# A decoder layer on Trainium2: the first feed-forward product turned token-major in ten groups, with seven block products for eight in two of eight k pairs

## The chip, the cores and the metric

The kernel runs on one core of a Trainium2 chip. The metric is the device time of one execution in microseconds. The engines are named as in the profile: PE is TensorE (PEld its weight loads), DVE is VectorE, ACT is ScalarE, POOL is GpSimd, SP is SyncE, whose queue issues the DMAs.

## The reference

One layer over 256 tokens of 2048 channels in float32: three token-mixing branches (attention, gMLP, S5) from one input projection, merged by gates, an output projection and a layer norm; then the feed-forward half that the change is about:

```python
gate_f, up = jnp.split(x @ w_ffn_in[l], 2, axis=-1)       # x (256, 2048), w_ffn_in (2048, 2 x 5632)
f = (jax.nn.silu(gate_f) * up) @ w_ffn_out[l]             # w_ffn_out (5632, 2048)
x = _layer_norm(ALPHA * x + f, ln2_g[l], ln2_b[l])
```

## The kernel before

**Split numbers.** Each float32 factor is cut into a high part (rounded to fp32r) and a low part (the remainder), and a product is made of three fp32r products: high x high, high x low, low x high. ScalarE makes the high part of a weight block (`split_h`, L262), VectorE the remainder (`split_l`, L268). Activations are kept as tiles of 512 columns for a k block of 128 channels: 256 tokens high, then 256 tokens low (`xT`, `x1T`, `h`).

**Units.** All work with weights is a list of `Unit`s of up to 1024 weight columns (8 k blocks x 128, or 2 x 512). The loop at L1210 goes through them: split the high parts of units up to four ahead (`advance`, four buffers `wh` and four `wl`), issue the unit's products, then its `post`, deferred steps and one step of each running task, then the remainders of what was split (`remainders`), each of which lets `top_up` issue a further weight load on SP (`load`, L251; four buffers `raw`). So every engine's order is fixed by this loop: a unit's split waits for the unit four before it to be multiplied, and a load for the remainder that frees its buffer. Engines work through their queues in order.

**Two forms of product.** `wide` (L79, L80) gives the output channel-major: the weights are the stationary tile, the activations move; for each k block one product of 512 columns (high weights x high and low tokens) and one of 256 (low weights x high tokens). `tall` (L165 to L167) gives it token-major: 128 tokens of an activation are the stationary tile and 512 columns of weights move; three products of 512 columns for each k block and half of the tokens. `w_v`, `w_o` and the second feed-forward product are `tall`; the gates and the first feed-forward product are `wide`.

**First feed-forward product.** 44 blocks f of 128 channels, each with a gate and an up tile of 16 k blocks, in two units each. The first four tiles run in `quad_tiles` (L108, L111) while the first layer norm ends, the other 84 through `wide`. `post_f1` adds the two halves of the bank (ScalarE, VectorE), makes silu x up and writes the split result into `h_tile(f)`: `h0` (f below 12, tag x24) or `h1` to `h10` (three f each, tag s6). `x1T` (tag t32) is the layer norm's result.

**Second.** Four column groups of `tall` over 44 k blocks, with `h` as the stationary tile. `ln2_load` runs ahead of its first unit and loads two rows of the norm, 1 MB each once spread over the partitions, into tag t32, where `x1T` was. The residual is read from `z` (tag t16, 2 MB), which the first layer norm left there.

**Places.** The pool's tags follow one another in each partition's memory, so a tile's start is fixed by what stands before it. By the built program xT, x1T, z, raw, wh, wl and h0 start 1632 bytes past a multiple of 2048 (32 past a multiple of 64), all tiles of tag s6 (m, h1 to h10, ...) 1728 past one, which is a multiple of 64. PSUM has four banks of tag mm and four of tag sd.

## Time and profile before

| | us |
|---|---|
| three runs, median (lowest, highest) | 1602.92 (1602.57, 1603.49) |
| the profiled execution | 1604.32 |
| its span, first to last instruction | 1602.6 |
| PE, DVE, ACT, POOL busy | 1580.8, 931.0, 763.8, 559.9 |
| first feed-forward product, `wide` tiles | 868.7 to 1343.5 |
| second feed-forward product | 1343.6 to 1589 |

The terms of a change are stage times within the span; the execution has 1.7 us around it, and the median of the runs stands 1.4 us below the profiled one. A row of the timeline is start, duration, engine, line, operation; products are pipelined, so the time of one is the distance between starts, not its duration.

### The profile page before, as it was taken

What the parts mean: (1) busy time and instruction counts of PE and PEld (TensorE: products, weight loads), DVE (VectorE), ACT (ScalarE), POOL (GpSimd) and SP (SyncE); (2) the same over time, 40 slices, a digit from 0 to 9 for tenths busy, and PEclk for the clock granted to TensorE, in tenths of its full rate; (3) what the DMA queues carried; (4) which work ended last, traced back from release to release, by engine and by line L of the source; (5) the groups of instructions that cost most, each with busy time, mean ns of one, the idle gap of its engine ahead of it and who ended that gap; (6) DMA issues with size and microseconds to landing.
All of it is one profiled execution on the core that took longest, in us unless ns stands there. A gap on an engine that the chain in (4) does not pass through costs nothing.

```text
span 1602.6 us, 24113 instructions
## 1 busy us (share of the span) xinstructions
PE 1580.8 (99%) x9094; PEld 1366.3 (85%) x9094; DVE 931.0 (58%) x1232; ACT 763.8 (48%) x1040; POOL 559.9 (35%) x1147
## 2 busy tenths in 40 slices
PE   8999999999999999999999999999999999999996
PEld 7888888898999998889789888888888888888885
DVE  5444555556855565469667556565555555445455
ACT  5444434456544444475444545554444544333342
POOL 7569999933999999203011000000000000000002
PEclk9999999999999999999999999999999999999998
DMA  8575557655656555557863565555555556666663
GB/s 275 176 251 186 187 203 207 155 148 188 211 188 198 194 184 194 178 164 209 286 222 118 190 193 184 184 184 184 186 185 192 183 193 237 204 187 192 186 188 101
DMA packets 106492, 307.50 MB, mean 192 GB/s; under 512 B 27567, under 2 KB 28079, under 8 KB 106120
## 3 DMA queue, kind: packets, MB, share of 16 engines
q1 hardware_dynamic: 106280, 305.82, 59.7%
q8 instruction: 71, 1.16, 0.3%
q14 instruction: 45, 0.37, 0.1%
q0 software_dynamic: 96, 0.15, 0.0%
HBM read 303.78 MB, written 5.53 MB: 193 GB/s over the span
## 4 chain that ended last, share of the span: by engine, by line
PE 94%; DVE 3%; DMA 1%; ACT 1%; issue 0%; POOL 0%; SPq 0%; POOLq 0%; ACTq 0%
PE ps_mm L79 40%; PE ps_mm L80 20%; PE ps_mm L165 9%; PE ps_mm L166 9%; PE ps_mm L167 9%; DVE wl L268 1%; PE ps_mm L857 1%; PE ps_mm L858 1%; PE ps_mm L856 1%; PE ps_sd L522 1%; PE ps_sd L691 1%; PE ps_mm L108 0%; PE ps_mm L111 0%; PE ps_sd L670 0%; DMA ln<-in_ln_g_dram 0%
## 5 line engine op out<-in xcount | busy, mean ns | idle before, releaser
L268 DVE TENSOR_TENSOR wl<-raw,wh 128x1024 fp32r<-128x1024 f32 (+1 forms) x544 | 654.2, 1227 | 167.1 <-ACT wh L262 166.6
L262 ACT ACTIVATE wh<-raw 128x1024 fp32r<-128x1024 f32 (+1 forms) x544 | 556.7, 1024 | 369.1 <-PE ps_mm L167 171.6
L79 PE MATMUL ps_mm<-xT,wh 128*128 128x512 f32 x1344 | 480.6, 400 | 6.6 <-ACT wh L58 5.9
L79 PE MATMUL ps_mm<-x1T,wh 128*128 128x512 f32 x1344 | 474.9, 399 | 0.0
L80 PE MATMUL ps_mm<-xT,wl 128*128 128x256 f32 x1344 | 378.9, 282 | 0.5 <-DVE wl L268 0.5
L80 PE MATMUL ps_mm<-x1T,wl 128*128 128x256 f32 x1344 | 377.5, 281 | 0.0
L79 PEld LDWEIGHTS ps_mm<-xT,wh 128*128 128x128 f32 x1344 | 254.3, 189 | 67.1 <-ACT wh L58 5.9
L79 PEld LDWEIGHTS ps_mm<-x1T,wh 128*128 128x128 f32 x1344 | 252.6, 188 | 63.0
L937 POOL TENSOR_TENSOR z<-z,ln2w 128x512 f32<-128x512 f32 (+1 forms) x4 | 5.2, 1302 | 732.5 <-ACT z L936 732.5
L80 PEld LDWEIGHTS ps_mm<-xT,wl 128*128 128x128 f32 x1344 | 256.1, 191 | 1.5 <-DVE wl L268 0.8
L80 PEld LDWEIGHTS ps_mm<-x1T,wl 128*128 128x128 f32 x1344 | 253.9, 189 | 0.0
L546 POOL TENSOR_TENSOR X<-X,t 128x48 f32<-128x48 f32 x255 | 129.1, 506 | 48.6 <-ACT X L526 48.6
L544 POOL TENSOR_TENSOR t<-s5keep,X 128x48 f32<-128x48 f32 x254 | 126.6, 498 | 44.5 <-ACT X L526 24.7
L547 POOL TENSOR_TENSOR X<-X,t 128x48 f32<-128x48 f32 x255 | 129.9, 509 | 20.0
L166 PE MATMUL ps_mm<-wl,h 128*128 128x512 f32 x340 | 134.1, 394 | 0.0
L165 PE MATMUL ps_mm<-wh,h 128*128 128x512 f32 x340 | 134.1, 394 | 0.0
L167 PE MATMUL ps_mm<-wh,h 128*128 128x512 f32 x340 | 134.1, 394 | 0.0
L1037 DVE TENSOR_TENSOR tmp<-ps_mm,tmp 128x256 f32<-128x256 f32 x88 | 37.3, 424 | 152.9 <-ACT tmp L1036 152.9
L545 POOL TENSOR_TENSOR t<-s5keep,X 128x48 f32<-128x48 f32 x254 | 108.5, 427 | 0.0
L315 ACT ACTIVATE tmp<-ps_mm,bcol 128x256 f32<-128x256 f32 x90 | 42.7, 474 | 137.6 <-PE ps_mm L80 137.4
L1036 ACT ACTIVATE tmp<-ps_mm 128x256 f32<-128x256 f32 x88 | 33.8, 384 | 151.6 <-PE ps_mm L80 151.6
L165 PEld LDWEIGHTS ps_mm<-wh,h 128*128 128x128 f32 x340 | 64.0, 188 | 15.0
(214 smaller groups left out, 1775.6 us busy)
## 6 DMA issues: line engine op xcount, KB each, us to landing
raw<-in_w_f_dram SPq DMA_DIRECT2D x264, 512.0 KB, 4.3
raw<-in_w_b_dram SPq DMA_DIRECT2D x164, 512.0 KB, 4.6
raw<-in_w_o_dram SPq DMA_DIRECT2D x32, 512.0 KB, 5.0
raw<-in_w_v_dram SPq DMA_DIRECT2D x24, 512.0 KB, 4.0
raw<-in_w_p_dram SPq DMA_DIRECT2D x32, 384.0 KB, 3.4
raw<-in_w_zv_dram SPq DMA_DIRECT2D x16, 384.0 KB, 3.6
tmp<-tab SPq DMA_DIRECT2D x64, 64.0 KB, 3.2
raw<-in_w_p_dram SPq DMA_DIRECT2D x16, 256.0 KB, 2.9
```

Of the source, the lines that this page charges most:

```text
L79: T.matmul(ps, lhsT=h[:, j * 128:(j + 1) * 128], rhs=a, start=k == 0, stop=last, skip_group_check=True)
L80: T.matmul(ps[:, 0:256], lhsT=l[:, j * 128:(j + 1) * 128], rhs=a[:, 0:256], start=False, stop=last, skip_group_check=True)
L165: T.matmul(ps[:, :n], lhsT=ah, rhs=hs, start=k == 0, stop=False)
L166: T.matmul(ps[:, :n], lhsT=ah, rhs=ls, start=False, stop=False)
L167: T.matmul(ps[:, :n], lhsT=al, rhs=hs, start=False, stop=k == total - 1)
L262: A.activation(h[:, :m], raws[n][:, :m], AF.Copy)
L268: V.tensor_tensor(l[:, :m], raws.pop(n)[:, :m], h[:, :m].bitcast(F32), op=ALU.subtract)
L315: A.activation(t, ps[:, 256:512], AF.Identity, bias=bcol[:, col:col + 1], scale=scale)
L544: G.tensor_tensor(t1, keep[:, 0], prev, op=ALU.mult)
L545: G.tensor_tensor(t2, keep[:, 1], prev[:, :, ::-1], op=ALU.mult)
L546: G.tensor_tensor(cur, cur, t1, op=ALU.add)
L547: G.tensor_tensor(cur, cur, t2, op=ALU.add)
```

## The change

Blocks f 4 to 43 (ten groups of four) are computed token-major by `seven`; f 0 to 3 stay as they were. A group has eight bank-sized results of 128 tokens x 512 channels or sums of such. In k pairs 0, 1, 2, 5, 6, 7 the eight block products (gate and up, two halves of the tokens, two k blocks) are made as in `tall`, three products each. In pairs 3 and 4 a seven-product scheme runs: VectorE makes sums of the four weight blocks (`combine`: four operations of 512 columns) and, once, of x1T's blocks (`sums`, tile `S`), and seven block products are accumulated in banks 1 to 7; `evict` after pair 4 takes out banks 1, 7, 6, 5 and `gates_` and `ups` add the rest. A pair has four units: g and u (loaded, 1024 columns), t1 (512) and tt (1024), which are sums and have no load. The banks of a group are split over tags mm and sd by turns. `turns` transposes the gated result in the next group (four transposes and one split for each half of the tokens, after its units 3 and 4). `S` takes the place of `z`, which is sent to DRAM and read back in `ln2_load`. A load now takes four runs of 1 KB from each partition's row in place of one of 4 KB. A constant `pad` of 320 bytes, and the S5 integers moved before it, make x1T, S, raw, wh, wl, h0 and all tiles of tag s6 start on multiples of 2048.

TensorE, first feed-forward product, before: weights `wh`, `wl` as stationary tile, x1T moving, by k block:

```order
L79 MATMUL ps_mm<-x1T,wh 128x512
L80 MATMUL ps_mm<-x1T,wl 128x256
L79 MATMUL ps_mm<-x1T,wh 128x512
L80 MATMUL ps_mm<-x1T,wl 128x256
L79 MATMUL ps_mm<-x1T,wh 128x512
```

The same place after, end of unit g to tt of a group's first pair (`S` the sums of x1T, ps the output bank):

```order
L1134 MATMUL ps_sd<-wh,x1T 128x512
L1135 MATMUL ps_sd<-wh,x1T 128x512
L1136 MATMUL ps_sd<-wl,x1T 128x512
L1134 MATMUL ps_mm<-wh,S 128x512
L1135 MATMUL ps_mm<-wh,S 128x512
L1136 MATMUL ps_mm<-wl,S 128x512
L1134 MATMUL ps_sd<-wh,S 128x512
L1135 MATMUL ps_sd<-wh,S 128x512
L1136 MATMUL ps_sd<-wl,S 128x512
L1134 MATMUL ps_mm<-wh,S 128x512
```

The weights have become the moving tile, and each block is three products of 512 columns.

VectorE, before, one pair of gate and up tiles (L268 the remainders of the units to come, the others the tile's end):

```order
L1037 TENSOR_TENSOR tmp_12776<-ps_mm,tmp_12776 128x256
L1046 SCALAR_TENSOR_TENSOR tmp_12779<-tmp_12779,tmp_12776 128x256
L268 TENSOR_TENSOR wl<-raw,wh 128x1024 x2
L1037 TENSOR_TENSOR tmp_12827<-ps_mm,tmp_12827 128x256
L1050 TENSOR_TENSOR tmp_12779<-tmp_12779,tmp_12827 128x256
```

VectorE, after, in a late group, from the turned halves of the group before (L66) to the remainder of tt (L301 with tt, 1024 columns):

```order
L66 SCALAR_TENSOR_TENSOR h_11065<-ps_mm,h_11065 128x2x128
L301 TENSOR_TENSOR wl<-raw,wh 128x1024
L66 SCALAR_TENSOR_TENSOR h_10709<-ps_mm,h_10709 128x2x128
L66 SCALAR_TENSOR_TENSOR h_11065<-ps_mm,h_11065 128x2x128
L301 TENSOR_TENSOR wl<-raw,wh 128x1024
L301 TENSOR_TENSOR wl<-tt,wh 128x512
L292 TENSOR_TENSOR tt<-raw 128x512
L293 TENSOR_TENSOR raw<-raw 128x4x128
L294 TENSOR_TENSOR tt<-raw 128x512
L295 TENSOR_TENSOR tt<-raw,tt 128x512
L301 TENSOR_TENSOR wl<-tt,wh 128x1024
```

The second pair's four sums (L292 to L295) stand ahead of the remainder that the first pair's tt products need.

SP, after, from the four `wide` tiles to the second product (L262 weight loads, zd the copy of z in DRAM):

```order
L262 DMA raw<-in_w_f_dram 128x1024 x12
L1101 DMA zd<-z 128x2048 x2
L262 DMA raw<-in_w_f_dram 128x4x256 x160
...
L1271 DMA z<-zd 128x2048 x2
L1275 DMA ln2w<-in_ln_g_dram 128x2048
L1275 DMA ln2w<-in_ln_b_dram 128x2048
```

z leaves ahead of the groups' loads and comes back ahead of the norm's two rows, on the one queue.

```diff
--- before.py
+++ after.py
@@ -39,6 +39,10 @@
     V, A, G, T = nc.vector, nc.scalar, nc.gpsimd, nc.tensor
 
     RAW_BUFS, HL_BUFS, AHEAD = 4, 4, 4
+    PAD = 80
+    PAIRS = (3, 4)
+    SP = len(PAIRS)
+    FIRST, LAST = 1, 10
 
     def bank(tag="mm"):
         return psp.tile([128, 512], F32, tag=tag, bufs=4, name=f"ps_{tag}")
@@ -63,8 +67,10 @@
 
 
...
@@ -247,8 +253,14 @@
 
         def load(n):
             u = units[n]
+            if u.role in ("t1", "tt"):
+                return
             r = raw_tile()
-            nc.sync.dma_start(r[:, :u.k * u.n], u.src)
+            if u.role:
+                u.pair[u.role] = r
+            dst = r[:, :u.k * u.n]
+            nc.sync.dma_start(dst if len(u.src.shape) == 2 else dst.rearrange("p (f c) -> p f c", f=u.src.shape[1]),
+                              u.src)
             raws[n] = r
 
         def split_h(n):
@@ -259,13 +271,36 @@
             else:
                 h = sb.tile([128, 1024], F32R, tag="wh", bufs=HL_BUFS, name="wh")
                 l = sb.tile([128, 1024], F32R, tag="wl", bufs=HL_BUFS, name="wl")
+            if u.role == "g" and "t" not in u.pair:
+                combine(u.pair)
+            elif u.role == "t1":
+                raws[n] = u.pair["t"][:, 0:512]
+            elif u.role == "tt":
+                raws[n] = u.pair["t"][:, 512:1536]
+                if u.pair["next"]:
+                    combine(u.pair["next"])
             A.activation(h[:, :m], raws[n][:, :m], AF.Copy)
             hl[n] = rest[n] = (h, l)
 
+        def combine(p):
+
+            p["t"] = s6([128, 1536], F32, "tt")
+            b = [p[e][:, 0:1024].rearrange("p (f k c) -> p k f c", f=4, k=2) for e in "gu"]
+            b11, b21, b12, b22 = b[0][:, 0], b[0][:, 1], b[1][:, 0], b[1][:, 1]
+            t1, t2, t4 = (p["t"][:, 512 * i:512 * i + 512].rearrange("p (f c) -> p f c", f=4) for i in range(3))
+            V.tensor_tensor(t1, b12, b11, op=ALU.subtract)
+            V.tensor_tensor(b12, b22, b12, op=ALU.subtract)
+            V.tensor_tensor(t2, b12, b11, op=ALU.add)
+            V.tensor_tensor(t4, b21, t2, op=ALU.subtract)
+
         def split_l(n):
-            m = units[n].k * units[n].n
+            u = units[n]
+            m = u.k * u.n
             h, l = rest.pop(n)
             V.tensor_tensor(l[:, :m], raws.pop(n)[:, :m], h[:, :m].bitcast(F32), op=ALU.subtract)
+            if u.role not in ("t1", "tt"):
+                pos["raw"] -= 1
 
         pos = {}
 
@@ -284,7 +319,12 @@
 
         def top_up():
             seq = pos["seq"]
-            if pos["load"] < len(seq) and pos["load"] - pos["l"] < RAW_BUFS:
+            if pos["load"] < len(seq):
+                u = units[seq[pos["load"]][0]]
+                if u.role not in ("t1", "tt"):
+                    if pos["raw"] >= RAW_BUFS:
+                        return False
+                    pos["raw"] += 1
                 load(seq[pos["load"]][0])
                 pos["load"] += 1
                 return True
@@ -301,6 +341,8 @@
...
+        s5["i"] = const.tile([128, NJ], I32, name="s5i")
+        const.tile([128, PAD], F32, name="pad")
 
 
...
         def s5_setup():
             P = s5["P"]
-            PI = sb.tile([128, NJ], I32, tag="s5i", bufs=1, name="s5i")
+            PI = s5["i"]
             keep = const.tile([128, 3, NJ, 2], F32, name="s5keep")
             bm = s6([128, 2, NJ, 32], F32, "bm")
             bb = s6([128, 2, NJ, 32], F32, "bb")
@@ -1024,7 +1066,7 @@
                     big["h0"] = sb.tile([128, 12, 512], F32R, tag="x24", bufs=1, name="h0")
                 return big["h0"][:, f, :]
             i = (f - 12) // 3
-            if (f - 12) % 3 == 0 and ("h", i) not in big:
+            if ("h", i) not in big:
                 big["h", i] = s6([128, 3, 512], F32R, f"h{i}")
             return big["h", i][:, (f - 12) % 3, :]
 
@@ -1051,6 +1093,157 @@
                     y = h_tile(f)
                     copy_split(y[:, 0:256], y[:, 256:512], w, 0.5)
             return post
+
+        def first_sums():
+
+            big["zd"] = dram.tile([128, 2, D], F32, name="zd")
+            for t in range(2):
+                nc.sync.dma_start(big["zd"][:, t, :], big["z"][:, t, :])
+            spawn(sums())
+
+        def sums():
...
+            big["S"] = sb.tile([128, 4, SP, 256], F32R, tag="t16", bufs=1, name="S")
+            for s in range(4):
+                o = big["S"][:, s]
+                copy_split(o[:, :, 0:128], o[:, :, 128:256], sr[:, s])
+                if s % 2:
+                    yield
+
...
+        def three(ps, a, h, l, start, stop):
+            T.matmul(ps, lhsT=a[0], rhs=h, start=start, stop=False)
+            T.matmul(ps, lhsT=a[1], rhs=h, start=False, stop=False)
+            T.matmul(ps, lhsT=a[0], rhs=l, start=False, stop=stop)
+
+        def seven(g):
+
+            P = {}
+            tags = ("mm", "sd") if g % 2 == 0 else ("sd", "mm")
+
+            def cols(w, j):
+                return w.rearrange("p (f k c) -> p k f c", f=4, k=2)[:, j]
+
+            def prod(n, a, h, l, start, stop):
+                if n not in P:
+                    P[n] = bank(tags[n in (1, 5, 6, 7)])
+                three(P[n], a, h, l, start, stop)
+
+            def mk(role, i):
+                def mm(h, l):
+                    z = 2 * PAIRS[i]
+                    ends = i == 0, i == SP - 1
+                    if role == "g":
+                        prod(1, act2(0, z), cols(h, 0), cols(l, 0), *ends)
+                        prod(2, act2(0, z + 1), cols(h, 1), cols(l, 1), False, False)
+                    elif role == "u":
+                        prod(7, act_s(2, i), cols(h, 0), cols(l, 0), *ends)
+                        prod(3, act_s(3, i), cols(h, 1), cols(l, 1), False, False)
+                    elif role == "t1":
+                        prod(5, act_s(0, i), h[:, 0:512], l[:, 0:512], *ends)
+                    else:
+                        prod(6, act_s(1, i), h[:, 0:512], l[:, 0:512], *ends)
+                        prod(4, act2(1, z + 1), h[:, 512:1024], l[:, 512:1024], False, False)
+                return mm
+
+            def mk8(up, i):
+                def mm(h, l):
+                    for t in range(2):
+                        for j in range(2):
+                            prod(((2, 4), (3, 8))[up][t], act2(t, 2 * i + j), cols(h, j), cols(l, j),
+                                 (i, j) == (0, 0), (i, j) == (7, 1))
+                return mm
+
+            def begin():
+                if g > FIRST:
+                    spawn(turns(g - 1))
+
+            def evict():
+                c = P["c"] = {n: tmp() for n in (1, 7, 6, 5)}
+                A.activation(c[1], P[1], AF.Copy)
+                V.tensor_tensor(c[6], P[6], c[1], op=ALU.add)
+                V.tensor_tensor(c[7], P[7], c[6], op=ALU.add)
+                V.tensor_tensor(c[6], P[5], c[6], op=ALU.add)
+                V.tensor_tensor(c[5], P[5], c[7], op=ALU.add)
+
+            def gates_():
+                c = P["c"]
+                P["w"] = [tmp(), tmp()]
+                for t, (n, m) in enumerate(((1, 2), (7, 4))):
+                    V.tensor_tensor(c[n], P[m], c[n], op=ALU.add)
+                    A.activation(P["w"][t], c[n], AF.Tanh, scale=0.5)
+
+            def ups():
+                c = P["c"]
+                for n, m in ((6, 3), (5, 8)):
+                    V.tensor_tensor(c[n], P[m], c[n], op=ALU.add)
+
+                def rest(t):
+                    w, a, b = P["w"][t], c[(1, 7)[t]], c[(6, 5)[t]]
+                    V.scalar_tensor_tensor(w, w, 1.0, a, op0=ALU.add, op1=ALU.mult)
+                    V.tensor_tensor(w, w, b, op=ALU.mult)
+                    if t == 0:
+                        later(lambda: rest(1), 0)
+                later(lambda: rest(0), 0)
+                big["w", g] = P["w"]
+
+            src = [d["w_f1"][8 * g + up:8 * g + 8:2].rearrange("f p k c -> p f k c") for up in range(2)]
+            pairs = [{} for _ in PAIRS]
+            for i, p in enumerate(pairs):
+                p["next"] = pairs[i + 1] if i + 1 < SP and g < LAST else None
+            for i in range(8):
+                s = [a[:, :, 2 * i:2 * i + 2, :].rearrange("p f k c -> p f (k c)") for a in src]
+                if i in PAIRS:
+                    e = PAIRS.index(i)
+                    pair = pairs[e]
+                    units.append(Unit(s[0], 8, 128, mk("g", e), role="g", pair=pair))
+                    units.append(Unit(s[1], 8, 128, mk("u", e), role="u", pair=pair))
+                    units.append(Unit(None, 4, 128, mk("t1", e), role="t1", pair=pair))
+                    units.append(Unit(None, 8, 128, mk("tt", e), role="tt", pair=pair,
+                                      post=evict if e == SP - 1 else None))
+                else:
+                    units.append(Unit(s[0], 8, 128, mk8(0, i), post=gates_ if i == 7 else None,
+                                      before=begin if i == 0 else None))
+                    units.append(Unit(s[1], 8, 128, mk8(1, i), post=ups if i == 7 else None))
+
+        def turns(g):
+
+            tag = "mm" if g % 2 == 0 and g < LAST else "sd"
+            for _ in range(3):
+                yield
+            for t in range(2):
+                ps = bank(tag)
+                for f in range(4):
+                    T.transpose(ps[:, f * 128:(f + 1) * 128], big["w", g][t][:, f * 128:(f + 1) * 128], ident)
+                f = 4 * g
+                while f < 4 * g + 4:
+                    n = min(4 * g + 4, 12 if f < 12 else f + 3 - f % 3) - f
+                    h_tile(f)
+                    y = big["h0"][:, f:f + n] if f < 12 else big["h", (f - 12) // 3][:, f % 3:f % 3 + n]
+                    copy_split(y[:, :, t * 128:(t + 1) * 128], y[:, :, 256 + t * 128:256 + (t + 1) * 128],
+                               ps.rearrange("p (f c) -> p f c", f=4)[:, f - 4 * g:f - 4 * g + n], 0.5)
+                    f += n
+                yield
 
...
         def ln2_load():
+            big["z"] = sb.tile([128, 2, D], F32, tag="t16", bufs=1, name="z")
+            for t in range(2):
+                nc.sync.dma_start(big["z"][:, t, :], big["zd"][:, t, :])
             w = sb.tile([128, 2, D], F32, tag="t32", bufs=1, name="ln2w")
+            spawn(turns(LAST))
             for i, nm in enumerate(("ln2_g", "ln2_b")):
                 nc.sync.dma_start(w[:, i, :], d[nm].partition_broadcast(128))
             big["ln2"] = w
@@ -1141,8 +1338,14 @@
                 f1.append(([d["w_f1"][2 * f + up, :, u * 8:(u + 1) * 8, :].rearrange("p k c -> p (k c)")
                             for u in range(2)], post_f1(f, up)))
         quad_tiles(f1[:4], act_x1, [home_x24(i) for i in range(3)] + [home_s6], ln1_hook)
-        for srcs, post in f1[4:]:
-            wide(srcs, 8, act_x1, post)
+        for i, (srcs, post) in enumerate(f1):
+            if 4 <= i < 8 * FIRST:
+                wide(srcs, 8, act_x1, post, before=first_sums if i == 4 else None)
+        for g in range(FIRST, LAST + 1):
+            seven(g)
+        for i, (srcs, post) in enumerate(f1):
+            if i >= 8 * LAST + 8:
+                wide(srcs, 8, act_x1, post)
         for g in range(4):
             tall([d["w_f2"][g, i].rearrange("p k c -> p (k c)") for i in range(22)], 2, 512, act_h, post_f2(g),
                  before=ln2_load if g == 0 else None, late=(lambda t, i: None) if g == 3 else None,
@@ -1203,7 +1406,7 @@
         for i in range(4):
             at = marks["o"] + 10 + 4 * i
             seq.insert(at + i, (first + i, at))
-        pos.update(load=4, h=4, l=4, live=4, seq=seq)
+        pos.update(load=4, h=4, l=4, live=4, raw=0, seq=seq)
         while top_up():
             pass
         marks["s5"] = spawn(s5_setup())
```

## Rows read from the trace of the kernel before

**Rows 1.** The page: busy us and instructions by engine; the chain by engine.
```profile
PE 1580.8 (99%) x9094; PEld 1366.3 (85%) x9094; DVE 931.0 (58%) x1232; ACT 763.8 (48%) x1040; POOL 559.9 (35%) x1147
...
PE 94%; DVE 3%; DMA 1%; ACT 1%; issue 0%; POOL 0%; SPq 0%; POOLq 0%; ACTq 0%
```
**Rows 2.** Both stages: us, PE, PEld, DVE, ACT, POOL busy, clock, DMA share, GB/s.
```profile
868.00:1343.00 475.00, 475.00 (x2693) 412.07 (x2692) 282.78 (x384) 238.28 (x340) 0.00 (x0) 1.00 0.58 187
1343.00:1589.00 246.00, 246.00 (x1061) 199.04 (x1059) 120.10 (x114) 93.75 (x91) 5.19 (x4) 1.00 0.61 190
```
**Rows 3.** L79: all starts in the first product; two from the gates' timeline.
```profile
L79 PE MATMUL ps_mm<-x1T,wh x1344: 395/398/403, 868.7 to 1343.3; 128*128 128x512 f32 x192
...
639.67 0.39 PE L79 MATMUL ps_mm<-xT,wh 128*128 128x512 f32 x1
...
659.78 0.39 PE L79 MATMUL ps_mm<-xT,wh 128*128 128x512 f32 x1
```
**Rows 4.** Timeline of PE: w_v, w_o, second product (h0, later h); L108.
```profile
210.19 0.39 PE L165 MATMUL ps_mm<-wh,xT 128*128 128x512 f32 x1
...
229.91 0.39 PE L165 MATMUL ps_mm<-wh,xT 128*128 128x512 f32 x1
...
784.99 0.40 PE L165 MATMUL ps_mm<-wh,m 128*128 128x512 f32 x1
...
802.57 0.39 PE L165 MATMUL ps_mm<-wh,m 128*128 128x512 f32 x1
...
1344.31 0.40 PE L165 MATMUL ps_mm<-wh,h 128*128 128x512 f32 x1
...
1359.96 0.39 PE L165 MATMUL ps_mm<-wh,h 128*128 128x512 f32 x1
...
1360.66 0.40 PE L165 MATMUL ps_mm<-wh,h 128*128 128x512 f32 x1
...
1380.34 0.40 PE L165 MATMUL ps_mm<-wh,h 128*128 128x512 f32 x1
...
847.45 2.08 PE L108 MATMUL ps_mm<-x1T,wh 128*128 128x256 f32 x16
```
**Rows 5.** Timeline of PE: four transposes between products of w_o.
```profile
837.47 0.39 PE L167 MATMUL ps_mm<-wh,m 128*128 128x512 f32 x1
837.70 0.60 PE L956 MATMUL ps_sd<-ident,z 128*128 128x128 f32 x4
838.05 0.48 PE L165 MATMUL ps_mm<-wh,m 128*128 128x512 f32 x1
838.37 0.40 PE L166 MATMUL ps_mm<-wl,m 128*128 128x512 f32 x1
```
**Rows 6.** VectorE's remainders: count, total us, mean ns; one of 512 columns.
```profile
L268 DVE TENSOR_TENSOR wl<-raw,wh 128x1024 fp32r<-128x1024 f32 x205 | 244.8, 1221 | 107.3 <-ACT wh L262 107.1
...
371.64 0.69 DVE L268 TENSOR_TENSOR wl<-raw,wh 128x512 fp32r<-128x512 f32 x1
```
**Rows 7.** Start of the second product: SP, ACT, and a window's row.
```profile
1347.60 0.42 SPq L1078 DMA_DIRECT2D ln2w<-in_ln_g_dram  x1
...
1349.33 1.06 ACT L262 ACTIVATE wh<-raw 128x1024 fp32r<-128x1024 f32 x1 [1.66 <-PE ps_mm L167]
1352.05 1.06 ACT L262 ACTIVATE wh<-raw 128x1024 fp32r<-128x1024 f32 x1 [1.66 <-PE ps_mm L167]
1357.85 1.06 ACT L262 ACTIVATE wh<-raw 128x1024 fp32r<-128x1024 f32 x1 [4.74 <-DMA raw<-in_w_f_dram]
...
1352.00:1355.00 3.00, 3.00 (x15) 2.47 (x14) 1.23 (x1) 1.06 (x1) 0.00 (x0) 1.00 0.97 408
```
**Rows 8.** DMA packets and the queue's share: 262 to 275 us, 900 to 1300.
```profile
DMA packets 4681, 2.27 MB, mean 174 GB/s; under 512 B 4384, under 2 KB 4384, under 8 KB 4681
...
q1 hardware_dynamic: 4681, 2.27, 74.1%
...
q1 hardware_dynamic: 20431, 74.42, 57.3%
```

More of the change, by code (lines that the diff above doesn't have):

```diff
@@ L65, in hybrid_layer, with __init__ @@
     class Unit:
-        def __init__(self, src, k, n, mm, post=None, before=None, uses=1, home=None, fence=False):
+        def __init__(self, src, k, n, mm, post=None, before=None, uses=1, home=None, fence=False,
+                     role=None, pair=None):
             self.src, self.k, self.n = src, k, n
+            self.role, self.pair = role, pair
             self.mm, self.post, self.before = mm, post, before
@@ new lines, in act2, with act_s @@
+        def act2(t, k):
+            a = big["x1T"][:, k, :]
+            return a[:, t * 128:(t + 1) * 128], a[:, 256 + t * 128:256 + (t + 1) * 128]
+        def act_s(s, i):
+            a = big["S"][:, s, i, :]
+            return a[:, 0:128], a[:, 128:256]
+        def three(ps, a, h, l, start, stop):
+            T.matmul(ps, lhsT=a[0], rhs=h, start=start, stop=False)
+            T.matmul(ps, lhsT=a[1], rhs=h, start=False, stop=False)
+            T.matmul(ps, lhsT=a[0], rhs=l, start=False, stop=stop)
@@ new lines, in turns @@
+        def turns(g):
+            tag = "mm" if g % 2 == 0 and g < LAST else "sd"
+            for _ in range(3):
+                yield
+            for t in range(2):
[10 more added lines that the diff above has]
+                    f += n
+                yield
```

10 lines of the change are left out of this document (added).

## The prediction

> **What bounds the kernel now.** I read the page's busy times first and the chain that ended last second. TensorE is busy 1580.8 of 1602.6 us and holds 94% of the chain [rows 1], so a microsecond is gained only where TensorE issues fewer or quicker products, and lost wherever another engine makes it wait. Then the two stages of the feed-forward half: in both TensorE is busy for the whole stretch, VectorE about 60% in the first (282.8 of 475) and half in the second, ScalarE half in the first, GpSimd idle in the first, DMA 58% and 61% [rows 2]. So TensorE's own rate sets both stages, and there is slack on the others. Third, that rate. In the first product a k step is one product of 512 columns and one of 256; 1344 steps start between 868.7 and 1343.3, so a step takes 474.6/1343 = 353.4 ns [rows 3]. For 512-column products by threes, the form that the change adopts, there are two rates [rows 4]: 29 triples lie between the two starts with xT as stationary tile and 23 between those with h0, which gives 226.7 and 226.8 ns a product; 25 with m and 28 with the later h tiles give 234.4 and 234.3. The moving tile is wh in all four. What differs is the address of the stationary one: xT and h0 start 32 bytes past a multiple of 64, as wh does; m and the h tiles of tag s6 start on one.
>
> **The ten groups' products.** Before: 80 tiles x 16 steps x 353.4 ns = 452.3 us. After: a group has 16 k x 2 token halves x 2 (gate, up) x 3 = 192 products of 512 columns, less 2 pairs x 3 for the eighth product left out: 186, and ten groups 1860. Their stationary tiles (x1T, S) and their moving one now all start on multiples of 2048, so they stand to each other as xT and h0 stood to wh; I take 226.7 ns: 421.7 us. The gain is 30.6 us, some 17 of it from the better rate and 14 from the 60 products fewer. Bounds: 234.3 ns gives 435.8 (gain 16.5); the 512 columns alone at 2.4 GHz (granted clock 1.00 [rows 2]) are 213.3 ns, 396.8 us. Most products read the moving tile as four runs of 128 columns; the nearest row, a product with two such runs, takes 2.08 us for 16 of 256 columns [rows 4], no more than the contiguous step, so I charge nothing.
>
> **Transposes.** The result is token-major and must be turned: 80 transposes in 20 batches of four. A batch of four with the product before and the one after it fills 0.90 us where two products fill 0.47 [rows 5]: 0.43 us each, 8.6 us, all on TensorE. None of it can hide.
>
> **VectorE.** A 1024-column remainder takes 1.22 us and a 512-column one 0.69 [rows 6]. A group needs 12 + 6 remainders of 1024 and 2 of 512, 8 sums of weight blocks, 4 sums at the evict, 4 + 4 in the rest, and the turned halves: some 39 us beside 42.2 + 0.9 us of TensorE. On average it fits, but it is not spread evenly. From a group's last product to the tt unit of the next group's first pair the order has, in a row on VectorE: two adds, four gating operations, 7 remainders of 1024, two combines of four (the second pair's stands ahead of the first pair's last remainder), one remainder of 512 and two turned halves, each in two pieces of 0.43. 15 x 0.69 + 7 x 1.22 + 2 x 0.86 = 20.6 us. TensorE covers the same stretch in 6 x 12 + 15 products and two batches: 87 x 0.2267 + 0.86 = 20.6 us. VectorE can only begin when the last product has landed and waits for ScalarE ahead of each second piece of a turned half, some 1.7 us in all (about 0.6 a piece, a ScalarE copy of the same size), so TensorE waits about 1.7 us there in seven groups, about 1.0 in the two whose halves are one piece, none in the first, which turns nothing: 14 us. Bounds: 0, if VectorE is let in earlier, and 33, if its chain is a tenth (2.1 us) longer. The rest of the group (evict, gates) falls behind full units of 2.7 us with one 1.22 us remainder each and costs nothing; without that cover it would add 2.8 us a group. ScalarE has 24 us a group and stays idle for over a third.
>
> **The sums of x1T, and z out and back.** first_sums sends z to DRAM, 2 MB, and the tile S takes its place, so ScalarE's first copy into S waits for that store; behind it on ScalarE stand the coming splits, behind those VectorE's remainders, and on SP the next weight loads. 2 MB at the 408 GB/s of [rows 7] is 5.1 us, some 7.5 with a weight load ahead and the landing; S is wanted after two units, 5.7 us. With 4.7 us of new VectorE work (one operation of 1024 and eight of 256 columns, 0.43 each by the line through the two of [rows 6]), against some 1.7 us that two units leave free there, I take 5.4 us; bounds 0 and 9. At the start of the second product ln2w's 2 MB already hold up a weight load: issued at 1347.6, they make ScalarE wait 4.74 us to 1357.85 for a load, where the rhythm of the splits before it (1349.33, 1352.05, so 2.72 apart) would have let it start at 1354.8 [rows 7]. It is 3.1 us late, with three units (8.2 us) less split and remainder (2.3) to spare, so 2.8 us are left. z's way back adds 5.1 us ahead of it on the same queue: 2.3 us of wait. Bounds 0 and 5.
>
> **Weight loads in runs of 1 KB.** Between 900 and 1300 the 74.42 MB are 18169 packets of 4 KB, and one takes 57.3% x 400 x 16 / 18169 = 0.20 us; between 262 and 275, taking the 297 large ones out, 4384 small ones of 256 bytes take 95 us, 0.022 each [rows 8]. A line through both gives 0.057 us for 1 KB, 14% more per byte than now: the DMA share of the stage goes from 0.58 to about 0.68. It hides; bound 0.2 us more wait in a group, 2 us.
>
> **Other stages.** w_o (384 products) and the second product's k steps from 12 on (768) have stationary tiles that now stand as h0 did: 1152 x 7.6 ns = 8.8 us gained; bounds 0 and, if aligned tiles are quicker still, 20. The older k steps outside the groups run at 353.4 or, in the gates, at 20.11 us for 58 steps, 346.7 ns [rows 3], with the same tiles at the same places; what chooses is not in the trace, so I keep them and add -3.6 to +5.4 us to the range (544 slow and 800 quick steps x 6.7 ns).
>
> A sentence of the Trainium skill speaks against this term: TensorE: Matmul & The Clock Gate, part 2, has two separate read ports and says that loading the next weights takes nothing from the running product, so the stationary tile's place should not matter. [rows 4] differ by 7.6 ns with nothing else changed, and I go by them; by the page the 8.8 us would not come and the sum would be -0.3 us (rival 3).
>
> **The sum.** -30.6 + 8.6 + 14 + 5.4 + 2.3 - 8.8 = -9.1 us. The profiled execution took 1604.3 us around its span of 1602.6; the runs' median is 1602.9, and the terms are stage times of that span, so 1602.9 - 9.1 = 1593.8 us.
>
> **Rivals.** (1) Every aligned product is slow, because a stationary tile on a multiple of 64 is what costs: for it speaks that m and h are the two that stand on one; against it that a quick tile is then the one that stands askew. Then 14.1 us of the first term go, the 8.8 don't come, w_v and h0 lose 288 x 7.6 ns each (4.4), and TensorE's stretch of 87 products grows by 0.66 us, which takes 5.9 off the waits: 1593.8 + 21.4 = 1615.2. (2) VectorE becomes the bound of the groups: operations that read two runs of a block or write in place, which no row shows, cost more than a plain one. A chain longer by 1.0 us a group (5%) eats the whole gain; by a tenth it is 1613. (3) The address does nothing: 1593.8 + 8.8 = 1602.6. (4) Aligned tiles are quicker than any row: 220 ns, halfway to the bare columns, on 3588 products is 24 us, of which VectorE gives back 5: 1575. The same page (part 2, back-to-back gap) has 215.7 ns for 512 columns of bf16; by that figure the time would be about 1563, an estimate. (5) No waits: VectorE, the store and z's return are covered, 1593.8 - 21.7 = 1572.
>
> **How the numbers follow.** Forecast 0.44, with a range of its own of 1586 to 1602; (1) 0.15, (2) 0.14, (3) 0.10, (4) 0.10, (5) 0.07. 1574 to 1617 leaves out half of (4), most of (5), a third of (1) and the upper end of (2), some 0.18. Faster by over 0.2% (below 1599.7; 0.2% is about what a measurement of this kernel can tell from no change): 0.40 from the forecast, (4), (5) and a little of (2) and (3), 0.61. Within: 0.15, most of (3) and the forecast's upper end. Slower: 0.24, from (1) and (2).
>
> **What would show it.** Starts of the new triples 227 ns apart, not 234; h and m products 227 in the second product and w_o. Four transposes in 0.35 us. A wait of 1 to 2 us for VectorE's remainder at the first pair's tt product of each group from the second on, none elsewhere in a group; DMA share below 0.75 there. About 5 us of wait among the four wide tiles ahead of the groups, and a wait for a weight load some 15 us into the second product. The prediction is wrong if the groups take over 45 us each, or under 42.

## The result: 0.6% slower

The changed kernel takes 1612.16 us in the median (1608.9 to 1613.84) against 1602.93, a ratio of 1.0057 with a 95% interval of 1.0045 to 1.0069. The forecast was 1593.8. The profiled execution took 1611.2 us around a span of 1609.4, 6.8 more than the span of before, and the accounts below are made between these two spans.

The page of the changed kernel, with the same lines as [rows 1]:

```profile
PE 1564.3 (97%) x8474; PEld 1335.7 (83%) x8474; DVE 1034.1 (64%) x1317; ACT 768.3 (48%) x990; POOL 558.7 (35%) x1147
...
PE 83%; DVE 7%; DMA 5%; ACT 2%; issue 2%; POOL 1%; SPq 0%; POOLq 0%; DVEq 0%; ACTq 0%
```

TensorE is busy 16.5 us less, and yet the time is longer: it holds 83% of the chain instead of 94, and VectorE and DMA hold 12% instead of 4. The time that was saved in products went into waits.

Where the waits are, by stretches (the last 7.7 us of the quad tiles with the four wide tiles, the ten groups, the second product; columns as in [rows 2]):

```profile
860.60:898.60 38.00, 32.49 (x194) 28.79 (x193) 22.72 (x37) 18.21 (x30) 0.00 (x0) 0.91 0.58 187
898.60:1350.50 451.90, 438.15 (x1934) 359.25 (x1933) 363.24 (x430) 228.27 (x264) 0.00 (x0) 0.99 0.61 187
1350.50:1595.40 244.90, 242.34 (x1065) 199.99 (x1063) 123.17 (x120) 94.16 (x93) 4.54 (x4) 0.99 0.61 197
```

The groups take 45.2 us each, as long as the 80 tiles took before. TensorE is idle at times in all three stretches, and the granted clock is below 1.00 in all three; before it was 1.00 in both stages [rows 2].

TensorE's rate came out as forecast. Pairs of starts in w_o (m), a group (x1T), the second product (a later h tile) and, last, the wide steps of the gates:

```profile
784.90 0.39 PE L171 MATMUL ps_mm<-wh,m 128*128 128x512 f32 x1
...
802.58 0.39 PE L171 MATMUL ps_mm<-wh,m 128*128 128x512 f32 x1
...
970.25 0.39 PE L1134 MATMUL ps_mm<-wh,x1T 128*128 128x512 f32 x1
...
989.97 0.39 PE L1134 MATMUL ps_sd<-wh,x1T 128*128 128x512 f32 x1
...
1439.85 0.39 PE L171 MATMUL ps_mm<-wh,h 128*128 128x512 f32 x1
...
1459.57 0.39 PE L171 MATMUL ps_mm<-wh,h 128*128 128x512 f32 x1
...
639.74 0.40 PE L85 MATMUL ps_mm<-xT,wh 128*128 128x512 f32 x1
...
659.88 0.40 PE L85 MATMUL ps_mm<-xT,wh 128*128 128x512 f32 x1
```

78 products in 17.68 us and twice 87 in 19.72 are 226.7 ns each, where m and h took 234.4 and 234.3 [rows 4]. But 57 wide steps of the gates now take 20.14 us, 353.3 ns, where [rows 3] has 58 in 20.11, 346.7. The change doesn't touch their code.

What TensorE waited for between 860 and 1345 us (us in total, times, longest):

```profile
PE ps_sd L1136 <- DVE wl L301: 8.0, 5, 1.9
PE ps_mm L1136 <- DVE wl L301: 5.7, 4, 2.0
PE ps_mm L86 <- DVE wl L301: 5.5, 2, 5.1
```

By the spacing of starts, the nine waits in the groups cost 15.2 us and the two among the wide tiles 6.1. Eight of the nine stand at the first pair's tt product of groups 2 to 9, one at the second pair's first product of group 10. One of them, on TensorE:

```profile
1142.03 0.39 PE L1135 MATMUL ps_sd<-wh,S 128*128 128x512 f32 x1
1144.35 0.50 PE L1136 MATMUL ps_sd<-wl,S 128*128 128x512 f32 x1 [1.94 <-DVE wl L301]
1144.69 0.39 PE L1134 MATMUL ps_mm<-wh,x1T 128*128 128x512 f32 x1
...
1145.49 0.63 PE L1134 MATMUL ps_sd<-wh,x1T 128*128 128x512 f32 x1
1145.92 0.63 PE L1135 MATMUL ps_sd<-wh,x1T 128*128 128x512 f32 x1
...
1148.05 0.63 PE L1134 MATMUL ps_sd<-wh,S 128*128 128x512 f32 x1
1148.48 0.48 PE L1135 MATMUL ps_sd<-wh,S 128*128 128x512 f32 x1
1148.80 0.39 PE L1136 MATMUL ps_sd<-wl,S 128*128 128x512 f32 x1
```

After the wait, from 1145.49 on, seven products start 0.43 us apart: the clock is at 1.2 GHz instead of 2.4, and 1.4 us are lost on top of the wait's 2.1. The same happens after the waits at 1050 and 1234, not after the other six. VectorE just before it:

```profile
1125.69 3.49 DVE L301 TENSOR_TENSOR wl<-raw,wh 128x1024 fp32r<-128x1024 f32 x3
1132.01 0.69 DVE L292 TENSOR_TENSOR tt<-raw 128x512 f32<-128x512 f32 x1 [2.83 <-DMA raw<-in_w_f_dram]
...
1140.29 0.69 DVE L292 TENSOR_TENSOR tt<-raw 128x512 f32<-128x512 f32 x1
...
1143.08 1.22 DVE L301 TENSOR_TENSOR wl<-tt,wh 128x1024 fp32r<-128x1024 f32 x1
```

VectorE works in order, and the first pair's sums stand in its row ahead of the turned halves and two remainders. They need the pair's second weight block, which has not landed: VectorE stands still for 2.83 us. Over the groups that is 28.7 us, ten times.

Among the wide tiles, ScalarE's copy into S and TensorE behind it:

```profile
886.17 0.72 ACT L62 ACTIVATE S<-sr 128x256 fp32r<-128x256 f32 x2 [7.91 <-DMA zd<-z]
...
883.09 0.39 PE L85 MATMUL ps_mm<-x1T,wh 128*128 128x512 f32 x1
888.57 0.58 PE L86 MATMUL ps_mm<-x1T,wl 128*128 128x256 f32 x1 [5.09 <-DVE wl L301]
888.95 0.63 PE L85 MATMUL ps_mm<-x1T,wh 128*128 128x512 f32 x1
...
892.74 0.40 PE L85 MATMUL ps_mm<-x1T,wh 128*128 128x512 f32 x1
```

Here too the products behind the wait are slow, eleven of them, and 1.7 us go with them.

### The profile page after: what moved, and what is told of

Its sections match the earlier page's. It is cut to its first block, busy times and chain, and to the rows that moved or that the text cites. A ratio compares the mean times of both kernels' runs of the same rounds, so it can differ in the third digit from the quotient of the medians.

```text
span 1609.4 us, 23090 instructions
## 1 busy us (share of the span) xinstructions
PE 1564.3 (97%) x8474; PEld 1335.7 (83%) x8474; DVE 1034.1 (64%) x1317; ACT 768.3 (48%) x990; POOL 558.7 (35%) x1147
## 4 chain that ended last, share of the span: by engine, by line
PE 83%; DVE 7%; DMA 5%; ACT 2%; issue 2%; POOL 1%; SPq 0%; POOLq 0%; DVEq 0%; ACTq 0%
PE ps_mm L85 20%; PE ps_mm L86 10%; PE ps_mm L172 8%; PE ps_mm L171 8%; PE ps_mm L173 8%; PE ps_sd L1136 4%; PE ps_mm L1136 4%; PE ps_sd L1134 3%; PE ps_mm L1134 3%; PE ps_sd L1135 3%; PE ps_mm L1135 3%; DVE wl L301 3%; DMA raw<-in_w_f_dram 3%; PE ps_mm L900 1%; PE ps_mm L899 1%
## 5 line engine op out<-in xcount | busy, mean ns | idle before, releaser
L301 DVE TENSOR_TENSOR wl<-raw,wh 128x1024 fp32r<-128x1024 f32 (+1 forms) x544 | 655.2, 1227 | 176.0 <-ACT wh L282 175.0
L586 POOL TENSOR_TENSOR t<-s5keep,X 128x48 f32<-128x48 f32 x254 | 130.0, 512 | 44.1 <-ACT X L568 24.3
L589 POOL TENSOR_TENSOR X<-X,t 128x48 f32<-128x48 f32 x255 | 128.3, 503 | 20.0
L588 POOL TENSOR_TENSOR X<-X,t 128x48 f32<-128x48 f32 x255 | 113.7, 446 | 49.1 <-ACT X L568 49.1
L587 POOL TENSOR_TENSOR t<-s5keep,X 128x48 f32<-128x48 f32 x254 | 119.4, 470 | 0.0
L1136 PE MATMUL ps_sd<-wl,x1T 128*128 128x512 f32 x270 | 106.2, 393 | 1.5 <-DVE wl L301 1.5
L1134 PE MATMUL ps_mm<-wh,x1T 128*128 128x512 f32 x270 | 107.0, 396 | 0.0
L1134 PE MATMUL ps_sd<-wh,x1T 128*128 128x512 f32 x270 | 106.8, 395 | 0.0
L1136 PE MATMUL ps_mm<-wl,x1T 128*128 128x512 f32 x270 | 106.5, 395 | 0.0
L1135 PE MATMUL ps_mm<-wh,x1T 128*128 128x512 f32 x270 | 106.0, 393 | 0.0
L1135 PE MATMUL ps_sd<-wh,x1T 128*128 128x512 f32 x270 | 106.0, 392 | 0.0
L172 PEld LDWEIGHTS ps_mm<-wl,h 128*128 128x128 f32 x340 | 64.2, 189 | 16.0 <-DVE wl L301 2.5
```

Source lines behind the costliest of these rows:

```text
L172: T.matmul(ps[:, :n], lhsT=ah, rhs=ls, start=False, stop=False)
L301: V.tensor_tensor(l[:, :m], raws.pop(n)[:, :m], h[:, :m].bitcast(F32), op=ALU.subtract)
L586: G.tensor_tensor(t1, keep[:, 0], prev, op=ALU.mult)
L589: G.tensor_tensor(cur, cur, t2, op=ALU.add)
L1134: T.matmul(ps, lhsT=a[0], rhs=h, start=start, stop=False)
L1135: T.matmul(ps, lhsT=a[1], rhs=h, start=False, stop=False)
```

## The experiments

All are compared with the kernel before on the same chip, whose medians there were 1601.96 to 1602.63.

**The tiles' places alone.** The kernel before with this edit:

```diff
+        s5["i"] = const.tile([128, NJ], I32, name="s5i")
+        const.tile([128, 80], F32, name="pad")
-            PI = sb.tile([128, NJ], I32, tag="s5i", bufs=1, name="s5i")
+            PI = s5["i"]
```

> The kernel before with nothing changed but the places of the tiles, as the change has them. Theory (the place of the stationary tile against the moving one sets a product's rate): the products of w_o with m and of the second product with the later h tiles start 227 ns apart instead of 234; 1152 x 7.6 ns = 8.8 us less, 1594 us. Rival (the rate comes from something else in the changed kernel): 234 ns stays, 1603 us.

1597.34 us, ratio 0.9969 (0.9956 to 0.9981). In w_o a product without a wait takes 227.1 ns on average (234.2 before), over the second product 226.7 (232.2), and that stage is 5.9 us shorter. So the place is the cause. But only 4.7 of the 8.8 us came: the stages ahead of w_o take 3.3 us more, because the gates' steps take 351 ns here between 390 and 620 us, and 347 before. That would leave 5.5. The execution that was profiled took 1601.1 us, and w_o as a whole takes 92.0 us in it, little less than the 92.6 before: two waits of 0.9 and 1.0 us beyond a product's time stand there, and eight products at half clock follow, 1.6 us lost:

```profile
773.67 0.49 PE L166 MATMUL ps_mm<-wh,m 128*128 128x512 f32 x1 [0.77 <-ACT wh L263]
774.93 0.50 PE L167 MATMUL ps_mm<-wl,m 128*128 128x512 f32 x1 [0.77 <-DVE wl L269]
...
775.74 0.63 PE L167 MATMUL ps_mm<-wl,m 128*128 128x512 f32 x1
776.16 0.63 PE L168 MATMUL ps_mm<-wh,m 128*128 128x512 f32 x1
```

Two starts with m after that:

```profile
785.29 0.39 PE L166 MATMUL ps_mm<-wh,m 128*128 128x512 f32 x1
...
802.97 0.39 PE L166 MATMUL ps_mm<-wh,m 128*128 128x512 f32 x1
```

78 products, 226.7 ns.

**The changed kernel without the new places** (s5i and pad taken out again).

> The changed kernel with its tiles put back to the places of before. Theory: the groups keep 227 ns (x1T, S and wh stand to each other as they did), w_o and the second product from k step 12 on go back to 234 ns: 8.8 us more, 1621 us. Rival (the place does nothing): 1612 us.

1615.92 us, ratio 1.0085 (1.0070 to 1.0100). The groups keep 227.3 ns, w_o takes 234.2 and the second product 232.3 again. It is 3.8 us slower than the change and not 8.8, for the gates' steps are quick again: 57 of them in 19.76 us, 346.7 ns.

```profile
639.94 0.39 PE L85 MATMUL ps_mm<-xT,wh 128*128 128x512 f32 x1
...
659.70 0.39 PE L85 MATMUL ps_mm<-xT,wh 128*128 128x512 f32 x1
```

**Only m and the later h tiles askew.** The kernel before with a pad of 104 words and s5i left in its old place: xT, x1T, wh, wl and h0 on multiples of 2048, the tiles of tag s6 96 bytes past one.

> The kernel before with xT, x1T, wh, wl and h0 on multiples of 2048 as in the first run, but m and the later h tiles 32 bytes past a multiple of 64. Theory (a product is quick when both tiles stand alike to 64, slow when they don't): 234 ns with m and the later h tiles, 227 with h0 and xT, the 8.8 us of the first run gone. Rival (only a stationary tile on a multiple of 64 beside a moving one that stands askew is slow): 227 ns everywhere, and the time of the first run.

1602.33 us, ratio 0.9997 (0.9988 to 1.0007): nothing is gained, as the theory has it. 75 products with m in 17.58 us are 234.4 ns:

```profile
785.09 0.40 PE L166 MATMUL ps_mm<-wh,m 128*128 128x512 f32 x1
...
802.67 0.39 PE L166 MATMUL ps_mm<-wh,m 128*128 128x512 f32 x1
```

Here the stationary tile stands askew and the moving one doesn't; before it was the other way round. What counts is how the two stand to each other.

**Copies into S later.**

```diff
-            yield
+            for _ in range(5):
+                yield
             big["S"] = sb.tile([128, 4, SP, 256], F32R, tag="t16", bufs=1, name="S")
```

> The changed kernel with the copies into S four units later, when z's store has landed. Theory: TensorE's 6.1 us of waits at 880 to 889 go and with them the 1.7 us that 11 products lose at half clock behind them: 7.8 us less, 1604.4 us. Rival (the store holds up whatever is next on ScalarE and SP wherever it stands): half of the wait stays, over 1608 us.

1604.92 us, 7.2 less than the change. From the first wide product to the groups it is 23.3 us instead of 30.3; the long wait and the half clock behind it are gone, one of 0.6 us remains:

```profile
860.60:892.80 32.20, 31.78 (x205) 28.50 (x204) 20.19 (x33) 17.09 (x29) 0.00 (x0) 1.00 0.67 226
```

**Reload in pieces.** z and the norm's weights come in 16 pieces of 512 columns, one a unit, from the third unit on:

```diff
-            for t in range(2):
-                nc.sync.dma_start(big["z"][:, t, :], big["zd"][:, t, :])
+        def pieces():
+            ...
+                    nc.sync.dma_start(big["z"][:, t, c:c + 512], big["zd"][:, t, c:c + 512])
+                    yield
```

> The changed kernel with z and the norm's weights loaded in 16 pieces, one a unit, instead of 4 MB at once at the start of the second product. Theory (the weight load queued behind the 4 MB makes the wait): the 3.0 us of waits at 1370 to 1374 and the 1.6 us of half clock behind them go, 1607.6 us. Rival (the last group's turned halves hold up ScalarE and VectorE there): 1612 us.

1604.28 us. The second product takes 240.1 us instead of 244.8, without a wait: 4.7 us, as expected. The rest of the gain is in the groups, 448.1 instead of 451.9 us: their nine waits are 14.7 us there, but only one is followed by half clock. Which of them are differs from run to run.

**Pairs 3 and 6 instead of 3 and 4, each pair's sums ahead of its own first block.**

```diff
-    PAIRS = (3, 4)
+    PAIRS = (3, 6)
-                p["next"] = pairs[i + 1] if i + 1 < SP and g < LAST else None
+                p["next"] = None
```

> The changed kernel with the seven-product pairs 3 and 6 instead of 3 and 4, each pair's weight sums made right ahead of its own use. Theory (VectorE has too much in one stretch, not too much in all): the nine waits of 0.6 to 2.2 us at the group starts, 15.2 us, go, and the 4.4 us of half clock behind three of them: 1592.6 us. Rival (VectorE is short of time over the whole group): the waits come back at the second pair's products, over 1606 us.

1601.65 us, ratio 0.9999 (0.9990 to 1.0009). The groups take 441.1 us, 10.8 less, and no half clock is left in them, but ten waits of 0.3 to 1.0 us remain, 7.3 together, all at the first pair. VectorE's own wait for the second block has grown, since now both pairs' sums stand there:

```profile
DVE tt L292 <- DMA raw<-in_w_f_dram: 53.8, 20, 3.2
```

My theory held for half of the waits. The 7.3 us that I then put down to VectorE's load were tried next.

**The sums on GpSimd** (the four operations of combine with G for V, on the run above).

> Pairs 3 and 6 as in the run before, with the eight weight sums of a group on GpSimd, which is idle there. Theory (what is left of the waits in the groups, 7.3 us, is VectorE's load): they go, 1594.4 us. Rival (GpSimd takes about 1.3 us for an operation of this size, four in a row 5.2 us against 2.8 on VectorE, and the sums come later than they are wanted): the waits grow, over 1602 us.

1626.51 us, 25 more: the rival. GpSimd's operations take 1.29 to 1.81 us on average (count, total, mean ns), and in the groups ScalarE waits 75.6 us in all for the second of the four (L293):

```profile
L292 POOL TENSOR_TENSOR tt<-raw 128x512 f32<-128x512 f32 x19 | 34.4, 1810 | 363.3 <-DMA raw<-in_w_f_dram 285.7 <-PE ps_sd L1136 53.8 <-DVE h L66 23.7
...
L293 POOL TENSOR_TENSOR raw<-raw 128x512 f32<-128x512 f32 x19 | 24.5, 1289 | 1.5
```

Of VectorE's remainders of the sums one form got longer too: those of 512 columns take 1284 ns on average, against 685 with the sums on VectorE, while those of 1024 stay at 1222 (1221):

```profile
L301 DVE TENSOR_TENSOR wl<-tt,wh 128x512 fp32r<-128x512 f32 x20 | 25.7, 1284 | 0.0
```

The Trainium skill (SBUF — State Buffer, "SBUF: two separate sides") has GpSimd and a VectorE operation with two inputs in SBUF take turns at one pair of ports. The longer remainder would agree with that, but no run here tests it, nor separates it from GpSimd's own pace in what the kernel lost.

**All mends, sums on GpSimd** (the late copies, the reload in pieces, and the run above).

> The late copies into S, the pairs apart with sums on GpSimd, and the reload in pieces together. Theory (the waits are separate, and their sum is what the change lost): 1612 less 7.8, 10.8, 7.3 and 4.6 us, some 1582 us. Rival (a wait taken away at one place comes back at another, TensorE being ahead of the weight stream): over 1592 us.

1614.7 us. From the first wide product to the groups it is 23.4 us and the second product takes 240.2, as in their own runs; the groups take 470.3. So the gains at those two places are separate and add up, and the sums on GpSimd spoil the groups.

**The sums later, on VectorE.** From here on they are issued at the split of the pair's second block, when it has been loaded:

```diff
-            if u.role == "g" and "t" not in u.pair:
+            if u.role == "u":
                 combine(u.pair)
```

> The changed kernel with pairs 3 and 4 as they are, each pair's weight sums issued ahead of the split of its second block instead of its first. Theory (the sums stand on VectorE before their second block has landed, 2.8 us of idling in a row with the turned halves and remainders, and that makes the wait at the tt product): the 15.2 us of waits and 4.4 us of half clock go, 1592.6 us. Rival (VectorE's work in that stretch is too much even without idling; the wait moves to the second pair): over 1603 us.

1612.83 us, with pairs 3 and 4: the theory fell. VectorE no longer waits for a load, and the wait at the tt product is gone; but 26 waits of 0.5 to 1.0 us stand in its place, 19 of them at the second pair's second block. ScalarE's copy of that block comes after two of the four sums, and these after the first pair's remainders:

```profile
1148.63 1.06 ACT L282 ACTIVATE wh<-raw 128x1024 fp32r<-128x1024 f32 x1 [3.68 <-DVE raw L293]
```

The groups take 454.3 us. None of these waits is followed by half clock. So the sums' wait for the load made the wait at the tt product, but taking it away alone gains nothing.

**All mends, pairs 3 and 6 and pairs 3 and 4.** Late copies into S, reload in pieces, sums later; once with pairs 3 and 6, once with 3 and 4.

> Sums issued later, pairs 3 and 6, the late copies into S and the reload in pieces, nothing on GpSimd. Theory: no wait is left from 860 us on; ten groups at 421.7 us of products, 8.1 of transposes and 1.2 of small steps, 431 us against 451.9, with 7.0 and 4.7 us from the other two: 1579 us, below the run with all eight products by the 12 us that its 60 products more take. Rival (pairs apart still wait at the first pair): over 1586 us.

> The same with pairs 3 and 4. Theory (with the idling gone the stretch of both pairs fits behind TensorE): as with 3 and 6, 1579 us. Rival (two pairs in a row take more of VectorE than TensorE gives time for): a wait at the second pair's tt product, over 1586 us.

With pairs 3 and 6 it is 1582.32 us, ratio 0.9873 (0.9858 to 0.9887): 20 us faster than before and 30 faster than the change. With pairs 3 and 4 it is 1600.98. So the full gain in the groups, 16.7 us, takes both, sums that don't wait for a load and pairs with units between them: the pairs apart alone gave 10.8 of it, the later sums alone none. The groups of the first, and all that TensorE still waits for from 860 us on:

```profile
890.24:1325.37 435.13, 432.65 (x1934) 355.70 (x1933) 363.85 (x434) 224.89 (x266) 0.00 (x0) 1.00 0.62 194
...
PE ps_sd L1138 <- DVE wl L301: 1.4, 4, 0.4
PE ps_mm L1138 <- DVE wl L301: 1.1, 3, 0.4
PE ps_mm L86 <- DVE wl L301: 0.5, 1, 0.5
```

435.1 us against 452.3; seven waits of 0.5 us are most of what is missing to the 431 expected.

**All eight products.** No pair by the scheme: no sums, no S, z stays in place (PAIRS empty; gates and ups read the banks directly).

> The changed kernel with all eight products in every k pair: token-major groups and the tiles' new places alone, no sums of weights, no tile S, z stays where it is. Theory (the rate and the places are the gain, the scheme brings its own waits): ten groups of 1920 x 226.7 ns = 435.3 us and 8.6 us of transposes without a wait, 452.3 before; with 3.6 us from w_o, 5.9 from the second product and 3.1 lost in the gates' steps some 1587 us. Rival (token-major waits for VectorE at the group starts even so): over 1595 us.

1590.65 us, ratio 0.9928 (0.9913 to 0.9942), with no wait at all in the groups and VectorE at 52% there:

```profile
891.66:1335.80 444.14, 444.14 (x1994) 367.44 (x1993) 231.94 (x234) 192.42 (x215) 0.00 (x0) 1.00 0.62 191
```

So token-major groups and the new places are worth 11 us, the scheme as the change has it, with z's way out and back, costs 21, and mended it is worth 8.

**The gates' steps.** In the stretch from 390 to 620 us a wide step takes 346.9 to 347.2 ns on average in the three kernels whose s6 tiles stand askew to wh (before, the changed one with old places, and m and h askew), and 351.0 to 351.3 in all others so far. In this stretch the products between the gates read s6 tiles as moving tiles. Two runs put those alone askew, by 32 bytes inside slots lengthened by 64; the lengthening moves the other s6 tiles to several multiples of 64:

```diff
-        return sb.tile(shape, dt, tag="s6", bufs=11, name=name)
+        t = sb.tile([128, 1552], dt, tag="s6", bufs=11, name=name)
+        at = 8 if name[:2] in ("ya", "yb") or name[:3] == "yc2" else 0
+        t = t[0:shape[0], at:at + math.prod(shape[1:])]
```

> The first run (the kernel before with the tiles' new places) with the moving tiles of the products between the gates, those that hold the three heads' results, 32 bytes past a multiple of 64 as all tiles of their pool stood to wh before; m and the h tiles stay on multiples of 64. Theory (products whose moving tile stands unlike wh leave the gates' wide steps in the quick state): 347 ns a step from 390 to 715 us instead of 351 to 353, w_o and the second product at 227 ns, some 3.3 us below the first run, 1594 us. Rival (another tile of the pool, or an earlier stage, sets the state): 351 to 353 ns stays, 1597 us.

> The same step on the run with all mends. Theory: 347 ns a step in the gates and 3.3 us below that run, 1579 us. Rival: no change, 1582 us.

1598.78 and 1584.02 us: neither gain came, and the 1.4 and 1.7 us more than without are too little to tell from none (ratios 0.9979, interval 0.9969 to 0.9988, against 0.9956 to 0.9981; 0.9886, 0.9871 to 0.9901, against 0.9858 to 0.9887). In the first, the way from the first head's first product to w_o takes 372.2 us, 374.5 without and 371.3 in the kernel before: 2.3 of the 3.2 us are back. From some 500 us on, where the second head's products begin, the gates' steps take 347 ns. Before that, with the first head's tiles, they take 352. By the built program the first head's stand 480 and 288 bytes past a multiple of 512, the second's 96, as all s6 tiles did to wh before. So the rate goes with these moving tiles, but not every askew place gives the quick one. The lengthened slots moved the other s6 tiles too, so that these tiles alone are the cause is not shown, and why is open. What was gained is lost again in w_o and the second product, 229.7 and 229.4 ns a product, where m and the h tiles now stand at several distances from wh. All of these are multiples of 64, so to stand alike to 64 bytes, as the theory of the run with only m and the later h tiles askew had it, is not enough. In the second product, six products with a tile on a multiple of 512, and six with one 64 bytes past it:

```profile
1424.76 0.39 PE L173 MATMUL ps_mm<-wh,h 128*128 128x512 f32 x1
...
1426.12 0.39 PE L173 MATMUL ps_mm<-wh,h 128*128 128x512 f32 x1
...
1441.28 0.39 PE L173 MATMUL ps_mm<-wh,h 128*128 128x512 f32 x1
...
1442.68 0.39 PE L173 MATMUL ps_mm<-wh,h 128*128 128x512 f32 x1
```

1.36 us and 1.40: 226.7 and 233.3 ns.

## Why the prediction was wrong

Most steps held, and the sum missed by 16 us of the span: -9.1 forecast, +6.8 measured. The time is inside the range of 1574 to 1617, but slower than before and not faster, and the prediction's own sign came: the groups take 45.2 us each, over 45.

- **Products.** Right: 1860 at 226.7 ns, [rows 4] read as a matter of place. By the mean of the starts, 227.4, some 1.2 us of small delays come on top.
- **Places.** Right, and shown by three runs: 234 becomes 227 ns in w_o and the second product, 2.8 and 5.9 us. What the prediction drew from the Trainium skill (TensorE: Matmul & The Clock Gate, part 2: loading the next weights takes nothing from the running product), that the place should not matter, does not hold for this kernel. Rivals 1, 3 and 4 fall with that, and rival 5 with the waits.
- **Transposes.** Right: 18 batches in the groups cost 8.1 us, 7.7 expected.
- **VectorE's wait at the tt product.** The forecast came out in count and size, and in place but for group 10, where the wait stands at the second pair's first product: 1.05 and 0.6 us in the two groups with halves in one piece, 1.75 to 2.2 in the six after, 15.2 with group 10 against 14. But the working behind it was off. In the stretch counted, of the group with the wait at 1142 (1120.3 to 1144.3), VectorE was busy 19.5 us, not 20.6, and idle 4.5, not 1.7, and 2.8 of those were the sums' wait for a load, which I did not see: I asked what stands ahead of the tt remainder on VectorE, but not what each operation there waits for. Size and place agreed by chance.
- **The sums of x1T.** 6.1 us of waits against 5.4; the store took up to 9.8 us from an issue to its landing, not 7.5.
- **The second product's start.** 3.0 us of waits against 2.3, at 1371 to 1374.
- **DMA in runs of 1 KB.** 0.61 and not 0.68 in the groups. It hid.
- **What failed, first:** each wait was priced at its own length. Behind five of them TensorE ran at half clock, 1.7 us after the store, 4.4 in three groups, 1.6 in the second product: 7.7 us, nearly half of the miss. The granted clock of 0.91 and 0.99 shows it, and the runs that took the waits away had 1.00 in the same stretches. The Trainium skill (TensorE: Matmul & The Clock Gate, part 1) has an idle array fall back to half its clock; the trace agrees behind these five, but of the nine waits in the groups six, of 0.6 to 2.2 us, were followed by the full clock.
- **What failed, second:** the gates' steps were put at no change, as having "the same tiles at the same places". xT and wh moved alike, but the tiles of the products between the gates moved against wh, and 3.1 us were lost. It stood in the range and not in the sum.
- The rest: 2.6 us by which the three waits were larger, some 2.9 of small delays in the groups (those between products and at the transposes among them; 1.3 are put down to nothing), and 0.6 gained more in w_o.

The time lies near that of rival 2, but VectorE is not the bound it speaks of: busy 80% in the groups, and no less in the run with all mends, which is 17 us faster there. No rival had waits that cost more than they last.

## What to carry to other kernels

Where an engine works in order, ask of each operation put into its row what it waits for itself: a sum issued one block too early stops everything behind it, though the engine has time on average. Here mending that alone gained nothing, since 26 shorter waits took the place of the nine; the work had to be spread as well. Take a wait of TensorE off the path before counting what a cheaper scheme saves; here the same arithmetic is 0.6% slower or 1.3% faster by which pairs it is used in and when its sums, copies and reload are issued. And look at where a stationary tile stands against its moving one: some hundred words put in front of the tiles were worth more than half of what seven products for eight gave.

## What the runs showed of the hardware

- A 512-column product's time depends on how its stationary tile stands to its moving one. By the distance in bytes to a multiple of 512 (wh on one; means by tile in the run with lengthened slots): 0 226.7 ns; 256 229; 192 and 448 229 to 230; 128 and 384 232; 64 and 320 232 to 233. The distances are by the built program. With 96 bytes it was 234 in either direction.
- The steps of a 512- and a 256-column product have two rates, 346.7 and 353.3 ns, with their own tiles unchanged. Which one holds goes with the moving tiles of other products between them, and lasts after these have ended (from 615 to some 690 us in the run with lengthened slots). The cause is open.
- In the groups, waits of TensorE up to 1.0 us were never followed by half clock (26 of them in one run), but two of 0.9 and 1.0 us, 1.3 us apart, were in w_o (774 us, the kernel before with the new places); of those of 1.6 to 2.3 us some were, for 7 or 8 products, and some not; the one behind the store, 4 to 5.4 us, was in each run that had it, for 8 to 17 products.
